# A two-layer hybrid block in fp32: order of the query projection, query transposes, start of the fill, and where the norm's sums of squares are kept

## The chip, the cores and the metric

One core of one Trainium2 chip runs the whole program. The metric is the device time of one execution in microseconds, the median over the runs of the kernel.

## The reference

Two layers run one after the other over 512 latent tokens and 256 context tokens of width 1024. Each layer makes a modulated RMS norm, one input projection whose columns go to three groups of heads, one output projection, and a gated feed-forward network:

```python
hx = ada_modulate(x, norm_mix, sh_m, sc_m)            # rms_norm(x)*gain*(1+scale)+shift
hc = ada_modulate(cx, norm_mix, csh_m, csc_m)
fx, nqx, nkx, nvx, gqx, gkx, gvx, ggx, gax = split_in(hx @ w_in)
y_fn = fourier_mix(fx, fnet_w)                        # Re(2-D DFT) per 64 channels, then @ fnet_w
qxh, kxh, vxh = rms_norm(heads(nqx), na_q_norm), rms_norm(heads(nkx), na_k_norm), heads(nvx)
y_na = na_latent(qxh, kxh, vxh, kch, vch, na_rpb)     # 6 heads x 64, window 8x16 on a 64-wide grid + context keys
y_gla, yc_gla = gla_mix(...)                          # gated linear attention, 4 heads, both directions
y = jnp.concatenate([y_fn, y_na, y_gla], axis=-1) @ w_out
x = x + g_m * y
x = x + g_f * swiglu(ada_modulate(x, norm_ffn, sh_f, sc_f), ffn_w1, ffn_w3, ffn_w2)
```

The context stream goes through the same steps in layer 0 alone (its queries see only context keys); the output is the latent stream after layer 1.

## The kernel before

Everything is fp32. A product of two fp32 operands is three matmuls, since each operand is split into a high and a low part (`mm3`, line 181: high by high, low by high, high by low). Weights come from memory as `raw` and are split into `whl` by ScalarE and VectorE or GpSimd (lines 195 and 189), eight row blocks of 128 for a width of 1024.

A layer goes through these stages, with one order of matmuls for each:

- **Input projections.** `group(...)` runs a token tile of 128 at a time through one group of columns, and hands the PSUM bank to an evacuation function. The last four calls (lines 821 to 824) make the gate g of the linear attention and k, v, q of the neighbourhood attention; `ev_scr` (line 720) evacuates them and stores each tile to a scratch in DRAM by SP (line 732). For g that is a tanh and two products, for v one ScalarE copy, for k and q the head norm of lines 704 to 718: square on ScalarE (`hsq`), sum over a head and a small scaling on VectorE (`hss`), the power of -1/2 on GpSimd (`hrs`), two multiplications on VectorE (`nst`). In layer 0 q has six tiles (latent and context), in layer 1 four. The modulation vectors of what follows (`adac`, line 192) are made on VectorE during the same time. A last projection (lines 827 to 853) makes the input of the Fourier part.
- **Front of the attention.** `load_heads` (line 879) loads k, then q, then v back from the scratch in the order of the window's blocks, as `kn`, `qn`, `vn`. `fourier()` (line 1032) makes the DFT. `stacks_of_heads` (line 908) transposes the first two heads of kn and then of qn on TensorE (line 924) and splits them into the stacks `st` on ScalarE and VectorE. It is called once (line 1119), after six (layer 1: three) steps of `fourier()`; the rest of the Fourier steps come behind it in the program, and the scheduler weaves the two together.
- **Attention.** The loop of lines 1270 to 1298 writes TensorE's order out by hand. A unit is a pair of heads and a block of 128 queries: 15 units in layer 0 (3 pairs, 5 blocks), 12 in layer 1 (3 pairs, 4 blocks). For each, the scores of unit n are issued, then the transposes of unit n-1's probabilities (line 1223), then `fill`, then pieces of the next pair's transposes (line 947), then the values of unit n-1. The softmax in between is VectorE's biased maximum (`mx`, line 1191), ScalarE's exponential, VectorE's reciprocal (`rcl`, line 1201) and scaling.
- **The fill.** `fill(us)` issues pieces of `wo`, the part of the output projection that doesn't depend on the attention: 3 matmuls a piece, one row of 5 row blocks, in layer 1 8 x 5 = 40 pieces of 512 columns. It holds a credit: each call adds 2.4 us in layer 0 or 2.3 in layer 1, and pieces are issued while the credit is positive, each taking off columns x 3 / 2400 us. The credit starts at -2.4, so nothing is issued at the first unit. What is left of `wo` at the end is issued before the rest of the output projection.
- **Output projection of the attention and the norm behind it.** `wb` (line 1265) adds the attention's part of the output projection and the gated residual, a stream and a row block at a time. After each, `norm_add` (line 363) squares the new row block on ScalarE (`nsq`) and adds it to the stream's running sum `nacc` in SBUF: for the first stream (layer 0: the 256 context tokens; layer 1: the first half of 256 latent tokens) on VectorE, for the second (layer 0: the 512 latent tokens; layer 1: the second half) on GpSimd. `norm_sums` makes the column sums by matmuls with ones (`a<-u,nacc`), then `nms`, the power `nrs` on GpSimd, the spread over the partitions (`ndg`), and the modulation (`nt`, `u`) for the feed-forward network, whose first matmuls are `b<-u,whl` and `a<-u,whl`.

TensorE's order is written out by hand in the attention and the output projection; elsewhere a scheduler fixes each engine's order at build time by the order of the program and its own priorities. DMA is issued by SP, one queue in program order.

Of the kernel before, what the change touches and what calls it, by code (L numbers as in the profile page):

```python
# [19 lines left out]
AF = mybir.ActivationFunctionType  # L20
ALU = mybir.AluOpType
# [4 lines left out]
KD = 8  # L26
# [116 lines left out]
def hybrid_kernel(tc, d, out, dbg=None):  # L143
    nc = tc.nc
    ctx = ExitStack()
    V, S, G, T = nc.vector, nc.scalar, nc.gpsimd, nc.tensor
# [41 lines left out]
    def tt(e, o, a, b, op):  # L188
        e.tensor_tensor(out=o, in0=a, in1=b, op=op)  # L189
# [4 lines left out]
    def act(o, i, f=AF.Identity, **kw):  # L194
        S.activation(out=o, in_=i, func=f, **kw)  # L195
# [164 lines left out]

        return products, finish

    def norm_add(acc, x, k, tp, e):

        if k == 0:
            act(acc, x, AF.Square)
            return
        sq = mk(tp, [128, TL], F32, "nsq", 2)[:, :x.shape[-1]]
        act(sq, x, AF.Square)
        tt(e, acc, acc, sq, ALU.add)  # L370

    def norm_acc(xs, n, tp, e):

# [77 lines left out]
    for l in range(DEPTH):  # L451
# [108 lines left out]
        def group(src, cols, specs, evac, together=0, w=None, ps=None, after=None):  # L560

            w = w or wgroup(src, cols)
            ps = ps or {}
            for n, (i, c0) in enumerate(specs):
                if n == len(specs) - together:
                    for m, (j, cj) in enumerate(specs[n:]):
                        ps[j] = dense("mbmbya")[:, :cols - cj]  # L570
                    for k in range(KD):
                        for j, cj in specs[n:]:
                            token_major(ps[j], w, j, cj, k)
                if i not in ps:
                    ps[i] = dense("mb" if l == 0 else "mbmby")[:, :cols - c0]
                    for k in range(KD):
                        token_major(ps[i], w, i, c0, k)
                tick()
                evac(i, ps[i])
                next(steps, None)  # L580
                next(steps, None)
                if after:
                    after()
# [236 lines left out]

        group(d["wg"][l, 1], 384, qonly, ev_scr("g"))
        group(d["wg"][l, 2], 384, both, ev_scr("k"), after=between)
        group(d["wg"][l, 3], 384, both, ev_scr("v"), after=between)
        group(d["wg"][l, 4], 384, qonly, ev_scr("q"), after=between)


        ze = [mk(zp, [128, 2, 258], F32R) for _ in range(2)]
# [80 lines left out]
        def stacks_of_heads(p):  # L908

            for src, gain in ((kn, None), (qn, qg)):  # L910
                n = 768 if ctx_q or gain is None else 512
                kinds = (0, 1) if gain is None else (2,)
                for hh in range(2):
                    for k in kinds:
                        stacks[0, hh, k] = mk(p, [128, n], F32R, f"st{hh}{k}")
                for (j0, nj) in ((0, 4), (4, 2)):
                    if src is qn and j0 and not ctx_q:
                        continue
                    c0 = 128 * j0 if src is qn else (128 * j0 + 256) % 768
                    sl = slice(c0, c0 + 128 * nj)  # L920
                    pss = [ps()[:, :128 * nj] for ps in (PB, PA)]
                    for j in range(nj):
                        for hh, ps in enumerate(pss):
                            T.transpose(ps[:, 128 * j:128 * j + 128], src[j0 + j][:, 128 * hh:128 * hh + 128], ident)
                    for hh, ps in enumerate(pss):
                        u = [stacks[0, hh, k][:, sl] for k in kinds]
                        if gain is None:
                            split(ps, u[0], u[1])
                        else:
                            act(u[0], ps, AF.Copy, scale=gain)  # L930
                            lo = u[0][64:128]
                            stt(lo, ps[64:128], gain[64:128], lo.bitcast(F32), ALU.mult, ALU.subtract)
# [182 lines left out]
        load_heads(nap, "v", vn)  # L1115
        for _ in range(6 if ctx_q else 3):
            next(fn)
        with tc.issue_after(last_mm[0]):
            stacks_of_heads(nap)
        for _ in fn:  # L1120
            pass
        fst.close()
# [11 lines left out]

        load_streams(range(3))

        credit = [-2.4]

        def fill(us):

# [159 lines left out]
        nst_ = ExitStack()  # L1300
        np0 = pool(nst_, f"fn{l}", "left")
        accs = [mk(np0, [128, TL], F32, "nacc", 2)[:, :st_[1](0).shape[-1]] for st_ in streams]
        engines = (V, G) if ctx_q else (V, G)
        with tc.manual_schedule(engines={mybir.EngineType.PE}):
            since = 0
            for mn, _ in wb:
                if mn is None:
                    continue
                m, n = mn
                norm_add(accs[n], streams[n][1](m), m, np0, engines[n])  # L1310
                if mn == (1, 0):
                    early_w = tc.cur_priority
                if since == (1 if ctx_q else 3):
                    sums = norm_sums((accs[0], accs[0].shape[-1]), np0)
                if since == (2 if ctx_q else 7):
                    rb = norm_spread(sums, np0)
                since += bool(since) or mn == (KD - 1, 0)
# [142 lines left out]
```

## Time and profile before

| what | value |
|---|---|
| median of three runs | 1687.62 us (1684.39 to 2008.04) |
| the profiled execution | 1687.75 us |
| its span (first to last instruction) | 1686.0 us |
| granted clock of TensorE, mean | 0.984 of 2.4 GHz |
| busy: PE, VectorE (DVE), ScalarE (ACT), GpSimd (POOL) | 1634.9, 925.9, 581.4, 236.9 us |
| read from and written to memory | 174.84 and 14.29 MB |

The difference between the execution and its span, 1.75 us, lies outside of the profiled instructions. The program is a single run through the two layers: layer 0's attention begins at about 290 us, layer 1's at about 1205 us. How long a matmul takes is seen in the trace at two levels of the granted clock, 1.0 (2.4 GHz) and 0.5 (1.2 GHz); a window's clock is the mean over it. In a timeline, a row's bracket holds the idle time of the engine just ahead of it and what released it. The mark u in names of tiles stands for several unnamed tiles: identity, ones, halves of an operand.

### The profile page before, as it was taken

The page shows a single profiled execution, that of the slowest core. Times are in us where ns is not written, and L with a number is a line of the kernel's source. Part 1 is how long each engine was busy: PE and PEld are TensorE (multiplying, and loading weights), DVE is VectorE, ACT ScalarE, POOL GpSimd, SP SyncE. Part 2 cuts the span into 40 slices and gives each one's busy share as a digit, 9 for nine tenths or more (in the row PEclk, how much of TensorE's full clock was granted, in tenths as well). Part 3 has the DMA queues.
Part 4 walks back from the last instruction along what each step waited for, and adds up shares of the span by engine and source line. Part 5 has one row for each costly group of instructions (what it writes and reads, how often), then busy time and mean ns, then how long its engine had stood idle before and what let it go on. Part 6 is the DMA issues. An engine that isn't in the chain of part 4 may idle for free.

```text
span 1686.0 us, 25086 instructions
## 1 busy us (share of the span) xinstructions
PE 1634.9 (97%) x9938; PEld 1415.1 (84%) x9938; DVE 925.9 (55%) x1680; ACT 581.4 (34%) x1030; POOL 236.9 (14%) x280
## 2 busy tenths in 40 slices
PE   6999999999999999999999999999899999999999
PEld 5888898787888888888888889899777888888887
DVE  6799875677755553454533443453577553344332
ACT  4474224444334311221122324832444432222220
POOL 0243331003212300000000011332102200000000
PEclk9999999999899999999999999999899999999999
DMA  9445535634133352342321311222763143223321
GB/s 339 156 153 166 185 104 170 186 91 133 41 122 124 119 186 96 126 153 85 125 63 55 120 46 40 94 91 73 202 166 111 51 138 100 95 86 107 100 86 52
DMA packets 79906, 199.68 MB, mean 118 GB/s; under 512 B 10344, under 2 KB 21164, under 8 KB 78764
## 3 DMA queue, kind: packets, MB, share of 16 engines
q1 hardware_dynamic: 79788, 198.07, 37.3%
q8 instruction: 78, 1.28, 0.3%
q14 instruction: 40, 0.33, 0.1%
HBM read 174.84 MB, written 14.29 MB: 112 GB/s over the span
## 4 chain that ended last, share of the span: by engine, by line
PE 87%; DMA 5%; DVE 3%; ACT 2%; issue 1%; SPq 1%; POOL 1%; ACTq 0%; DVEq 0%; POOLq 0%
PE a L181 29%; PE m L181 25%; PE b L181 21%; PE y L181 10%; PE b L1223 1%; DMA qn<-scr_q 1%; DVE u L192 1%; DVE whl L189 1%; DMA st<-qt 1%; DMA raw<-in_woa 1%; DMA kn<-scr_k 0%; DMA bias<-in_rpb 0%; DVE nacc L189 0%; DMA raw<-in_wg 0%; ACT ab L195 0%
## 5 line engine op out<-in xcount | busy, mean ns | idle before, releaser
L195 ACT ACTIVATE whl<-raw 128x1024 fp32r<-128x1024 f32 (+7 forms) x222 | 204.8, 928 | 386.3 <-PE a L181 140.0
L181 PE MATMUL m<-u,whl 128*128 128x512 f32 (+1 forms) x1278 | 264.8, 359 | 0.5 <-DVE whl L189 0.5
L189 DVE TENSOR_TENSOR whl<-raw,whl 128x1024 fp32r<-128x1024 f32 (+7 forms) x201 | 223.1, 1112 | 73.7 <-ACT whl L195 73.6
L181 PE MATMUL a<-u,whl 128*128 128x512 f32 (+1 forms) x1299 | 249.0, 348 | 2.9 <-ACT u L195 2.4
L181 PEld LDWEIGHTS m<-u,whl 128*128 128x128 f32 x1278 | 212.7, 192 | 33.8 <-issue 1.2
L181 PEld LDWEIGHTS a<-u,whl 128*128 128x128 f32 x1299 | 210.5, 191 | 34.4 <-ACT u L195 2.8
L181 PE MATMUL b<-u,whl 128*128 128x512 f32 (+1 forms) x915 | 184.9, 352 | 3.1 <-DVE whl L189 1.8
L181 PEld LDWEIGHTS b<-u,whl 128*128 128x128 f32 x915 | 152.2, 193 | 26.7 <-DVE whl L189 2.4
L192 DVE SCALAR_TENSOR_TENSOR adac<-adaw,u,adac 128x512 f32<-128x512 f32 x196 | 154.6, 810 | 35.9 <-DMA adaw<-in_adaw 34.5
L181 PE MATMUL b<-whl,u 128*128 128x384 f32 (+1 forms) x696 | 145.6, 344 | 1.8 <-DVE u L192 1.8
L181 PE MATMUL m<-whl,u 128*128 128x384 f32 (+2 forms) x672 | 139.7, 344 | 1.9 <-ACT u L195 1.9
L181 PEld LDWEIGHTS m<-whl,u 128*128 128x128 f32 x672 | 115.6, 188 | 16.3 <-issue 9.6
L181 PEld LDWEIGHTS b<-whl,u 128*128 128x128 f32 x696 | 121.6, 188 | 8.0 <-issue 3.3
L181 PE MATMUL a<-g,whl 128*128 128x512 f32 (+1 forms) x594 | 126.7, 370 | 0.0
L181 PEld LDWEIGHTS a<-g,whl 128*128 128x128 f32 x594 | 103.9, 189 | 19.4 <-DVE ft L192 0.8
L192 DVE SCALAR_TENSOR_TENSOR ft<-ft,a 128x512 f32<-128x512 f32 (+1 forms) x53 | 30.5, 575 | 99.7 <-ACT ft L195 65.2
L181 PE MATMUL y<-u,whl 128*128 128x512 f32 (+1 forms) x420 | 82.5, 349 | 0.1
L181 PEld LDWEIGHTS y<-u,whl 128*128 128x128 f32 x420 | 68.1, 189 | 12.1 <-issue 1.7
L181 PE MATMUL m<-g,whl 128*128 128x512 f32 (+1 forms) x396 | 77.8, 350 | 0.0
L189 POOL TENSOR_TENSOR nacc<-nacc,nsq 128x256 f32<-128x256 f32 (+1 forms) x21 | 21.0, 1002 | 391.4 <-ACT nsq L195 391.3
L181 PEld LDWEIGHTS m<-g,whl 128*128 128x128 f32 x396 | 64.7, 189 | 9.7
L181 PE MATMUL b<-g,whl 128*128 128x256 f32 (+1 forms) x396 | 72.5, 336 | 0.0
(217 smaller groups left out, 2015.2 us busy)
## 6 DMA issues: line engine op xcount, KB each, us to landing
raw<-in_w SPq DMA_DIRECT2D x104, 512.0 KB
adaw<-in_adaw SPq DMA_DIRECT2D x48, 512.0 KB
adaw<-in_adaw SPq DMA_DIRECT2D x64, 256.0 KB
raw<-in_wg SPq DMA_DIRECT2D x40, 384.0 KB
raw<-in_w SPq DMA_DIRECT2D x32, 448.0 KB
adaw<-in_ada SPq DMA_DIRECT2D x8, 1024.0 KB
st<-kt SPq DMA_DIRECT2D x32, 192.0 KB
raw<-in_woa SPq DMA_DIRECT2D x16, 320.0 KB
```

Source lines behind the costliest of these rows:

```text
L181: last_mm[0] = T.matmul(o, lhsT=l, rhs=r, start=start, stop=stop, skip_group_check=True).ins
L189: e.tensor_tensor(out=o, in0=a, in1=b, op=op)
L192: V.scalar_tensor_tensor(out=o, in0=a, scalar=s, in1=b, op0=op0, op1=op1)
L195: S.activation(out=o, in_=i, func=f, **kw)
L1223: T.transpose(ps[:, 128 * j:128 * j + 128], p[:, 128 * j:128 * j + 128], ident)
```

## The change

Four edits are made.

1. q is projected ahead of v. The call of `after=between`, which advances the linear attention's output by a step, goes along with each tile.
2. `stacks_of_heads` becomes a generator with a stop ahead of k and one ahead of q. The stacks of k are made where both were; two more steps of `fourier()` follow; then the stacks of q; then the rest of `fourier()`.
3. The credit of `fill` starts at 0.
4. The running sum of squares of the first stream (both streams in layer 1) is held in one PSUM bank and added up by VectorE; the last of the eight additions writes the sum to SBUF, where the matmul with ones reads it. In layer 0 the latent stream's sum stays with GpSimd in SBUF.

```diff
--- before.py
+++ after.py
@@ -360,14 +360,15 @@
 
         return products, finish
 
-    def norm_add(acc, x, k, tp, e):
-
+    def norm_add(acc, x, k, tp, e, ps=None):
+
+        part = acc if ps is None else ps
         if k == 0:
-            act(acc, x, AF.Square)
+            act(part, x, AF.Square)
             return
         sq = mk(tp, [128, TL], F32, "nsq", 2)[:, :x.shape[-1]]
         act(sq, x, AF.Square)
-        tt(e, acc, acc, sq, ALU.add)
+        tt(e, acc if k == KD - 1 else part, part, sq, ALU.add)
 
     def norm_acc(xs, n, tp, e):
 
@@ -820,8 +821,8 @@
 
         group(d["wg"][l, 1], 384, qonly, ev_scr("g"))
         group(d["wg"][l, 2], 384, both, ev_scr("k"), after=between)
+        group(d["wg"][l, 4], 384, qonly, ev_scr("q"), after=between)
         group(d["wg"][l, 3], 384, both, ev_scr("v"), after=between)
-        group(d["wg"][l, 4], 384, qonly, ev_scr("q"), after=between)
 
 
         ze = [mk(zp, [128, 2, 258], F32R) for _ in range(2)]
@@ -908,6 +909,7 @@
         def stacks_of_heads(p):
 
             for src, gain in ((kn, None), (qn, qg)):
+                yield
                 n = 768 if ctx_q or gain is None else 512
                 kinds = (0, 1) if gain is None else (2,)
                 for hh in range(2):
@@ -1115,8 +1117,15 @@
         load_heads(nap, "v", vn)
         for _ in range(6 if ctx_q else 3):
             next(fn)
+        first = stacks_of_heads(nap)
+        next(first)
         with tc.issue_after(last_mm[0]):
-            stacks_of_heads(nap)
+            next(first)
+        for _ in range(2):
+            next(fn)
+        with tc.issue_after(last_mm[0]):
+            for _ in first:
+                pass
         for _ in fn:
             pass
         fst.close()
@@ -1134,7 +1143,7 @@
 
         load_streams(range(3))
 
-        credit = [-2.4]
+        credit = [0.0]
 
         def fill(us):
 
@@ -1300,14 +1309,15 @@
         nst_ = ExitStack()
         np0 = pool(nst_, f"fn{l}", "left")
         accs = [mk(np0, [128, TL], F32, "nacc", 2)[:, :st_[1](0).shape[-1]] for st_ in streams]
-        engines = (V, G) if ctx_q else (V, G)
+        bank = PA()
+        sums_ps = (bank[:, 0:256], None) if ctx_q else (bank[:, 0:256], bank[:, 256:512])
         with tc.manual_schedule(engines={mybir.EngineType.PE}):
             since = 0
             for mn, _ in wb:
                 if mn is None:
                     continue
                 m, n = mn
-                norm_add(accs[n], streams[n][1](m), m, np0, engines[n])
+                norm_add(accs[n], streams[n][1](m), m, np0, V if sums_ps[n] is not None else G, sums_ps[n])
                 if mn == (1, 0):
                     early_w = tc.cur_priority
                 if since == (1 if ctx_q else 3):
```

TensorE around the front of layer 0's attention, before; `kn` and `qn` in the input are transposes for the stacks, `m<-whl,ab` and `y<-u,u` matmuls of the Fourier part, `a<-st,st` scores, `b<-u,p` transposes of the probabilities, `m<-u,whl` the fill.

```order
L924 MATMUL a_3327<-u_104,qn_625_3103 128x128
...
L924 MATMUL b_3300<-u_104,kn_619_3091 128x128
...
L181 MATMUL m_3360<-whl_3253,ab_663_3277 128x258
...
L181 MATMUL y_3350<-u_3174,u_2893 1x256 x3
...
L924 MATMUL b_3326<-u_104,qn_625_3103 128x128
...
L181 MATMUL m_3360<-u_3259,ab_681_3357 128x258 x2
...
L181 MATMUL m_3384<-u_3259,ab_681_3357 128x258 x2
...
L181 MATMUL m_3384<-whl_3256,ab_665_3293 128x256 x3
L181 MATMUL a_3441<-st_666_3296,st_674_3324 128x512
...
L181 MATMUL a_3484<-st_666_3296,st_674_3324 128x512
...
L1223 MATMUL b_3512<-u_104,p_3452 128x128 x4
...
L181 MATMUL m_3531<-u_3055,whl_3088 128x256 x9
```

The same place after the change:

```order
L926 MATMUL b_3300<-u_104,kn_622_3097 128x128
...
L926 MATMUL b_3314<-u_104,kn_623_3099 128x128
...
L181 MATMUL m_3384<-u_3259,ab_675_3331 128x258
...
L926 MATMUL b_3360<-u_104,qn_625_3103 128x128
L926 MATMUL a_3361<-u_104,qn_625_3103 128x128
...
L181 MATMUL m_3384<-u_3259,ab_675_3331 128x258 x2
...
L181 MATMUL a_3441<-st_666_3296,st_679_3358 128x512
...
L181 MATMUL m_3480<-u_3055,whl_3088 128x256 x9
...
L181 MATMUL m_3497<-u_3054,whl_3088 128x512 x6
...
L181 MATMUL a_3513<-st_666_3296,st_679_3358 128x512
...
L1232 MATMUL b_3541<-u_104,p_3452 128x128 x4
```

The qn transposes now stand behind the Fourier stage's matmuls into the first of the two banks, eight matmuls ahead of the first scores, and the fill stands between the first scores and the second, where before it followed the first transposes of probabilities.

SP's queue at the end of layer 1's projections, before (`scr_v` and `scr_q` are the scratches in DRAM, `kn` and `qn` the loads from them, `in_dftl` and `in_woa` tables and weights):

```order
L732 DMA scr_v_1539_9368<-nst_11109 128x384
...
L732 DMA scr_q_1540_9369<-nst_11191 128x512
...
L732 DMA scr_q_1540_9369<-nst_11263 128x512
...
L426 DMA raw_11462<-in_dftl 128x514
...
L1073 DMA pe_11526<-in_nyq 1x258
L732 DMA scr_q_1540_9369<-nst_11299 128x512
L888 DMA kn_1929_11441<-scr_k_1538_9367 128x1x512
...
L886 DMA kn_1933_11449<-scr_k_1538_9367 128x512
...
L426 DMA raw_11434<-in_woa 128x640
...
L890 DMA qn_1935_11453<-scr_q_1540_9369 128x1x512
```

The same place after the change:

```order
L733 DMA scr_q_1541_9370<-nst_11026 128x512
...
L733 DMA scr_v_1540_9369<-nst_11116 128x384
...
L733 DMA scr_v_1540_9369<-nst_11280 128x384
L427 DMA raw_11330<-in_wfx 128x512
...
L733 DMA scr_v_1540_9369<-nst_11308 128x384
L427 DMA raw_11463<-in_dftl 128x514
...
L1075 DMA pe_11527<-in_nyq 1x258
L889 DMA kn_1930_11442<-scr_k_1539_9368 128x1x512
...
L887 DMA kn_1934_11450<-scr_k_1539_9368 128x512
...
L427 DMA raw_11435<-in_woa 128x640
...
L891 DMA qn_1936_11454<-scr_q_1541_9370 128x1x512
```

The last store ahead of the loads of kn is now one of v; the stores of q are all further up.

VectorE in layer 1's norm, before (`nacc`: the running sum in SBUF; `nms`, `ndg`, `nt`: the steps behind it):

```order
L189 TENSOR_TENSOR nacc_12648<-nacc_12648,nsq_12668 128x256
...
L189 TENSOR_TENSOR nacc_12648<-nacc_12648,nsq_12675 128x256
...
L192 SCALAR_TENSOR_TENSOR u_11670<-y_12734,u_107,u_11670 128x256
...
L189 TENSOR_TENSOR nacc_12648<-nacc_12648,nsq_12731 128x256
L192 SCALAR_TENSOR_TENSOR u_11671<-a_12746,u_107,u_11671 128x256
...
L391 TENSOR_SCALAR nms_12777<-a_12774 128x2
...
L189 TENSOR_TENSOR whl_13209<-raw_13207,whl_13209 128x1024
...
L403 TENSOR_SCALAR ndg_12838<-u_104,nrs_12779 128x128
```

The same place after the change; `a_12651` is the PSUM bank of the sums:

```order
L189 TENSOR_TENSOR a_12651<-a_12651,nsq_12670 128x256
...
L189 TENSOR_TENSOR a_12651<-a_12651,nsq_12677 128x256
...
L192 SCALAR_TENSOR_TENSOR u_11671<-y_12736,u_107,u_11671 128x256
L189 TENSOR_TENSOR nacc_12649<-a_12651,nsq_12733 128x256
...
L189 TENSOR_TENSOR a_12651<-a_12651,nsq_12759 128x256
...
L189 TENSOR_TENSOR a_12651<-a_12651,nsq_12773 128x256
...
L189 TENSOR_TENSOR a_12651<-a_12651,nsq_12794 128x256
...
L192 SCALAR_TENSOR_TENSOR nt_12905<-u_11671,u_109,a_12839 128x256
...
L189 TENSOR_TENSOR a_12651<-a_12651,nsq_12808 128x256
L192 SCALAR_TENSOR_TENSOR u_12877<-nt_12905,u_107,u_12877 128x256
...
L189 TENSOR_TENSOR nacc_12650<-a_12651,nsq_12857 128x256
```

The first half's additions keep their places; those of the second half, which stood on GpSimd, now stand among the steps of the first half's modulation (`ndg`, `nt`, `u`), three of them ahead of `nt`.

## Rows read from the trace of the kernel before

**Rows 1.** The page: granted clock in 40 slices; shares of the chain that ended last.

```profile
PEclk9999999999899999999999999999899999999999
...
PE 87%; DMA 5%; DVE 3%; ACT 2%; issue 1%; SPq 1%; POOL 1%; ACTq 0%; DVEq 0%; POOLq 0%
```

**Rows 2.** Window by stage: busy us and instructions of each engine, granted clock, DMA share, GB/s.

```profile
185.00:230.00 45.00, 45.00 (x306) 40.17 (x306) 36.03 (x72) 9.64 (x18) 12.41 (x9) 1.00 0.57 178
```

**Rows 3.** Timeline of PE, 289 to 313 us: start, duration, instruction, idle before and releaser.

```profile
289.74 0.33 PE L924 MATMUL a<-u,qn 128*128 128x128 f32 x1 [1.56 <-DMA qn<-scr_q]
...
298.92 0.98 PE L181 MATMUL m<-whl,ab 128*128 128x256 f32 x6
...
305.79 2.16 PE L1223 MATMUL b<-u,p 128*128 128x128 f32 x8 [1.78 <-DVE rcl L1201]
...
307.60 5.40 PE L181 MATMUL m<-u,whl 128*128 128x256 f32 x21
```

**Rows 4.** Window of the attention's front in layer 0.

```profile
288.00:314.00 26.00, 20.08 (x112) 16.34 (x111) 15.04 (x37) 11.02 (x27) 1.76 (x6) 0.80 0.54 167
```

**Rows 5.** Timeline of PE, 1205 to 1229 us, layer 1.

```profile
1205.34 0.30 PE L924 MATMUL a<-u,qn 128*128 128x128 f32 x1 [2.57 <-DMA qn<-scr_q]
...
1217.63 2.08 PE L181 MATMUL a<-st,st 128*128 128x512 f32 x4 [1.57 <-DVE st L192]
...
1223.29 2.15 PE L1223 MATMUL b<-u,p 128*128 128x128 f32 x8 [1.02 <-DVE rcl L1201]
...
1225.09 3.79 PE L181 MATMUL m<-u,whl 128*128 128x512 f32 x12
```

**Rows 6.** Window of the attention's front in layer 1.

```profile
1204.00:1229.00 25.00, 20.16 (x72) 14.89 (x72) 13.63 (x33) 9.09 (x23) 1.20 (x4) 0.59 0.56 168
```

**Rows 7.** Timeline of DVE and SP around the last store of q, layer 1.

```profile
1183.97 0.55 DVE L709 TENSOR_REDUCE hss<-hsq 128x6 f32<-128x384 f32 x1 [0.91 <-ACT hsq L195]
...
1186.46 0.76 DVE L189 TENSOR_TENSOR nst<-y,hrs 128x256 f32<-128x256 f32 x2 [1.50 <-POOL raw L848]
...
1187.24 0.35 SPq L732 DMA_DIRECT2D scr_q<-nst  x1
...
1187.64 2.54 SPq L888 DMA_DIRECT2D kn<-scr_k  x4
```

**Rows 8.** Timelines of DVE, POOL and PE in layer 1's norm, and its window.

```profile
1300.67 4.94 POOL L189 TENSOR_TENSOR whl<-raw,whl 128x1024 fp32r<-128x1024 f32 x2 [0.40 <-ACT whl L195]
...
1303.67 2.22 DVE L189 TENSOR_TENSOR nacc<-nacc,nsq 128x256 f32<-128x256 f32 x1
...
1306.21 0.41 DVE L189 TENSOR_TENSOR nacc<-nacc,nsq 128x256 f32<-128x256 f32 x1
...
1308.65 0.98 PE L181 MATMUL a<-u,nacc 128*128 128x1 f32 x4 [2.33 <-DVE nacc L189]
...
1319.09 0.51 PE L181 MATMUL b<-u,whl 128*128 128x256 f32 x2 [0.87 <-ACT u L195]
...
1308.00:1317.00 9.00, 8.35 (x45) 8.35 (x46) 4.90 (x12) 5.00 (x9) 6.87 (x7) 0.62 0.40 138
```

**Rows 9.** Layer 0's norm: timelines of PE and DVE, one group of lines, one window.

```profile
407.06 1.21 PE L181 MATMUL a<-u,whl 128*128 128x256 f32 x8 [0.22 <-DVE whl L189]
...
421.56 2.08 PE L181 MATMUL b<-u,whl 128*128 128x256 f32 x8 [1.13 <-DVE whl L189]
...
395.49 0.42 DVE L189 TENSOR_TENSOR u<-y,u 128x256 fp32r<-128x256 f32 x1 [2.36 <-ACT u L195]
...
404.90 2.10 DVE L189 TENSOR_TENSOR whl<-raw,whl 128x384 fp32r<-128x384 f32 x1
...
L189 DVE TENSOR_TENSOR nacc<-nacc,nsq 128x256 f32<-128x256 f32 x7 | 7.3, 1043 | 3.5 <-ACT nsq L195 3.5
...
420.00:428.00 8.00, 6.83 (x29) 5.85 (x30) 4.72 (x10) 2.10 (x4) 2.20 (x4) 0.79 0.00 0
```

**Rows 10.** Timeline of PE, last fill of layer 1.

```profile
1287.87 2.99 PE L181 MATMUL m<-u,whl 128*128 128x512 f32 x12
```

## The prediction

> **What bounds the kernel now.** I read the page first. TensorE carries 87% of the chain that ended last [rows 1], so only three things can shorten the program: PE's remaining idle time, the time that it spends at the lower clock, and its work. The change takes no work from PE (same matmuls, other order). The line PEclk of the slices shows where the clock was lowered: slice 11 and slice 29, one place in each layer. Then I read the windows by stage, the way to see which stage has slack: in the queries' and values' projections of layer 0 (185 to 230 us) PE is busy for all of 45.00 us and VectorE for 36.03 [rows 2]; the windows of the two fronts and the two norms are taken up below. Last came the timelines of PE, DVE and SP at the four places that the change touches: the front of the attention in each layer, and the norm behind it in each layer.
>
> **Front of attention, layer 0.** PE stops four times between 288 and 314 us, first 1.56 us for a load of qn, last 1.78 us for the softmax (rcl); the fill of 21 matmuls, which takes 5.40 us there, could have stood in these gaps, but starts only behind the last of them, at 307.60 [rows 3]. The window shows 20.08 us busy of 26.00 at a granted clock of 0.80 [rows 4]: 2.4 GHz for most of it, 1.2 GHz for stretches behind the stops. At the full clock this work is 20.08 x 0.80 = 16.1 us, so the most that can be had is 26.0 - 16.1 = 9.9: 5.9 of idle, 4.0 of clock. On PE the change moves 6 transposes of kn and 28 small matmuls of the Fourier stage ahead of the 12 transposes of qn; six such matmuls take 0.98 us [rows 3], so this is some 4 to 5 us of work, against 1.56 us and a second wait of about 1 for the load, and the start credit of 0 lets 21 fill matmuls run right behind the first scores, which covers the softmax waits. What is late next: the first scores now follow the transposes by only 8 matmuls, some 1.3 us, where 16 stood before, and need the split of the same stacks, which cost a bare wait of 1.57 us in layer 1 [rows 5]. I put about 1 us there. If the loads of qn still land too late, only the softmax waits and their share of the clock go, about half of the 9.9, or 5. Ends 5 and 9.9; value 8, near the row's own total less the new wait.
>
> **Front of attention, layer 1.** The same, deeper: stops of 2.57 (qn), 1.57 (st), 1.02 (rcl) and two small ones, then the fill's 12 matmuls take 3.79 us, where 12 of the same form take 2.99 at full clock later on [rows 5, 10]. The window 1204 to 1229 has 20.16 us busy of 25.00 at a clock of 0.59 [rows 6], so 11.9 us of work and at most 13.1 us to gain. Here the loads decide. The stores of q close the projections: behind the last product stand square, sum (hss 0.55), POOL's power and two multiplications (0.76 us) before the store of q at 1187.24, and SP issues the first load of kn only behind it, at 1187.64 [rows 7]. With v last, one ScalarE copy stands there, so kn, and qn behind it, can start about 3 us sooner, and q was stored long before. On PE the qn transposes also move back, by some 2.6 us of work. The waits of 2.57 and two small ones for qn ended with the last load near 1210 us, so 3 + 2.6 us covers most of it and not surely all. The wait of 1.57 for the split stays, since the scores still stand right behind the transposes. So at best 13.1 - 1.6 - 0.5 = 11. If the kn loads are held by something else than the store (they reuse memory of the stage before), the wait is only renamed, the clock falls again, and about 5.1 is left. Ends 5.1 and 11; value 8.5, between.
>
> **Norm behind the attention, layer 1.** VectorE's adds of squares run at 2.22 us while GpSimd runs weight splits of 2.5 us each (4.94 for two), and at 0.41 when it doesn't; PE waits 2.33 us for the last of them, and the window 1308 to 1317 then has a clock of 0.62 [rows 8]. That is 2.33 + 8.35 x 0.38 = 5.5 us. With the sum in PSUM the add should cost what a VectorE operation with one PSUM operand of the same size costs, 0.42 [rows 9], also beside GpSimd. Against that, the seven adds of the second half move from GpSimd to VectorE (7 x 0.42 = 2.9), and by the order three of them now stand ahead of the first modulated tile, on which the feed-forward's first matmul waits already for 0.87 us [rows 8]: 1.3 us later. Lower end 0 (the adds wait for ScalarE's square anyway, or PSUM adds are no faster), upper 5.5; value 4.0.
>
> **Norm behind the attention, layer 0.** Only the context's sum moves (7 adds of 128x256). Before, they take 7.3 us, the group's sum, where 7 x 0.42 = 2.9 would do, and five PE waits of 0.22 to 1.13 us, 2.9 together, all behind VectorE's or ScalarE's weight splits, follow; the window 420 to 428 has 6.83 busy at 0.79, another 1.4 [rows 9]. Ends 0 and 4.3; value 2.3, since part of the delay is the weight splits' own: one of 128x384 took 2.10 us [rows 9], while GpSimd was busy, and the latent stream's sum stays on GpSimd in SBUF. The Trainium skill's page "SBUF — State Buffer", section "Who interferes with whom", says that a VectorE operation with two SBUF inputs and a GpSimd operation that reads SBUF block each other for a whole instruction, and one with a single SBUF input does not. The trace agrees for the adds (2.22 against 0.41). The rule speaks against the full gain here: the splits have two SBUF inputs and keep their GpSimd neighbour. By it the term would be about 1.2, and the sum 1.1 less.
>
> **What the change costs.** (1) The fill has 0 for its start, so it is used up sooner. Layer 1 has 40 pieces of 0.64 us by the kernel's own count, 25.6 in all, and 12 blocks that ask for 2.3 each from the first on, 27.6; so they are gone one block early, and the 12 matmuls (2.99 us) that stand between the last scores and the last values [rows 10] are missing there: PE waits for the last softmax, about 2 us, with a drop of the clock possible. Ends 1 and 5; value 2. Layer 0 loses its last 9 matmuls ahead of the output projection, and waits for the split that ends with the 0.42 us operation at 395.49 [rows 9]: 0.5, ends 0 and 1. (2) In layer 0 six head norms of q (hss and two multiplications, 0.55 + 0.76, with the small scaling about 1.45 us on VectorE each) come into 185 to 230 us: 36.0 + 8.7 = 44.7 of 45.0 us [rows 2, 7]. That nothing waits rests on this being just enough. Ends 0 and 3; value 0.8. (3) SP: the last store moves by three places and four loads of qn start sooner: nothing.
>
> **Sum.** 8 + 8.5 + 4.0 + 2.3 - 2 - 0.5 - 0.8 = 19.5 us. The profiled execution took 1687.75 (span 1686.0 and 1.75 around it), 0.13 over the median of 1687.62. 1687.6 - 19.5 = 1668.1.
>
> **Rivals.**
> A, the waits are renamed. The loads of qn and kn end as late as now, PE stands at the moved transposes, and the clock falls there. For it: both fronts show DMA as releaser of the first stop; the landings in layer 1 go on to about 1210. Against it: in layer 0 the transposes move further than the stop was long. Both fronts at their lower ends: 5 + 5.1 + 6.3 - 3.3 = 13.1, so 1674.5.
> B, the norms give nothing. Each add waits for ScalarE's square, and in layer 1 the seven extra adds keep VectorE as late as it was. For it: VectorE stood idle for 3.5 us ahead of layer 0's seven adds, all of it behind a square [rows 9]. Against it: the 2.22 us adds of layer 1 had their squares long before. 8 + 8.5 - 3.3 = 13.2, less 1 for the late modulation: 1675.4.
> C, slower than before. VectorE in 185 to 230 us has 0.3 us of slack left and is fed by loads and by ScalarE, so it cannot fill every gap: the modulation of the next stage and the head norms fall behind, PE's banks are not emptied, and PE, which now never stops there, stands for the whole 8.7 us, then runs at 1.2 GHz for some 20 us (10 us lost), and the late q pushes back the front of the attention, whose 8 us then don't come. 19.5 - 8 - 8.7 - 10 + 0.8 = -6.4: 1694. It decides once VectorE's lag costs PE over 5 us, because then the clock goes too. For it: 44.7 of 45. Against it: from 230 us on VectorE is lightly used, and the next stage's modulation can slip there.
>
> **How the numbers follow.** Forecast 0.58, A 0.24, B 0.12, C 0.06. The forecast's own range is 1668 with about 8 to each side from the ends of the two fronts. Range for all: 1654 (both fronts and the norms near their upper ends, 9.9 + 11 + 9.8 - 1 = 29.7, which would be 1658, and some more for clock that I counted in no term) to 1684 (A and B together give 6.8, less a clock drop at the end of layer 1, 3). 2% of the time, about what a measurement of this kernel can tell from no change, is 33.8 us, which is more than all upper ends together: faster 0.05, within 0.92, slower 0.03 (C with more than one stretch at the lower clock).
>
> **What would show it.** Right: PEclk near 9 in slices 11 and 29; no wait for qn and rcl on PE at either front; fill matmuls straight behind the first scores; layer 1's adds at about 0.42 beside GpSimd's splits and no stop of 2.33 us ahead of the sums' matmuls; a wait of 1 to 3 us for p or rcl in layer 1's last block. Wrong: PE idle in layer 0 between 185 and 230 us (C); a stop at the moved transposes with DMA as releaser (A); adds still at 1 us or more, or a longer stop at the first feed-forward matmul (B).

## Result, and the profile after

The kernel after the change takes 1667.43 us (median of four runs, 1664.77 to 1668.75), 0.9888 of the kernel before, with a 95% interval of 0.9868 to 0.9909; the ratio leaves out the one slow run of the kernel before, at 2008.04 us. By that ratio it is 18.9 us faster, 15.3 to 22.3; run once more as a control beside the experiments it came to 0.9898 [0.9878, 0.9919]. The profiled execution took 1666.35 us, its span is 1664.3. The forecast was 1668.1.

The page after, against [rows 1]: no slice of PEclk is below 9 any more. (The chain of the page is not compared: it breaks off early in this trace and covers some 30% of the span.)

```profile
PE   6999999999999999999999999999999999999999
...
PEclk9999999999999999999999999999999999999999
```

The windows after, moved to where the same work now stands: the projections of q and v in layer 0, the front in each layer, then the norm in layer 1 and in layer 0, against [rows 2, 4, 6, 8, 9].

```profile
185.00:230.00 45.00, 45.00 (x305) 39.92 (x305) 42.05 (x95) 10.08 (x19) 19.47 (x15) 1.00 0.59 190
286.00:312.00 26.00, 22.03 (x141) 18.46 (x140) 16.48 (x41) 12.09 (x30) 1.76 (x6) 0.93 0.65 198
1191.00:1216.00 25.00, 21.11 (x125) 17.20 (x126) 18.10 (x39) 13.51 (x31) 0.86 (x4) 0.93 0.67 195
1289.00:1298.00 9.00, 7.47 (x61) 7.06 (x60) 8.01 (x20) 5.27 (x11) 2.24 (x2) 1.00 0.70 227
414.00:422.00 8.00, 7.33 (x44) 6.29 (x43) 5.75 (x13) 3.19 (x7) 3.56 (x3) 1.00 0.09 32
```

Most of what the fronts gained is clock: 0.80 to 0.93 and 0.59 to 0.93. Idle time fell less, from 5.9 to 4.0 us in layer 0 and from 4.8 to 3.9 in layer 1. The timelines say where it stands. Layer 0's front, PE and then DVE; the first row lies ahead of the window:

```profile
283.95 0.33 PE L926 MATMUL a<-u,kn 128*128 128x128 f32 x1 [0.96 <-DMA kn<-scr_k]
...
297.62 1.25 PE L181 MATMUL a<-st,st 128*128 128x512 f32 x4
298.70 3.42 PE L181 MATMUL m<-u,whl 128*128 128x256 f32 x21
...
302.32 1.17 PE L181 MATMUL a<-st,st 128*128 128x512 f32 x4
307.16 1.00 PE L1232 MATMUL b<-u,p 128*128 128x128 f32 x4 [3.67 <-DVE p L1211]
```

```profile
303.24 0.69 DVE L189 TENSOR_TENSOR kt<-b,kt 128x512 fp32r<-128x512 f32 x1 [0.20 <-ACT kt L195]
305.56 0.48 DVE L192 SCALAR_TENSOR_TENSOR u<-m,u,u 128x256 f32<-128x256 f32 x1 [1.63 <-DMA u<-in_cxt]
305.96 0.15 DVE L1210 RECIPROCAL rcl<-sml 128x1 f32<-128x1 f32 x1
```

The two stops for qn are gone, and the fill of 21 matmuls stands right behind the first scores as written, in 3.42 us where it took 5.40 [rows 3]. But a new stop of 3.67 us follows, and a transpose of kn now waits 0.96 us for its load, which none did before. Read the DVE rows: the residual addition of the fill's own first product (`u<-m,u,u`) waits 1.63 us for a load of the context stream, and the reciprocal of the softmax, which PE waits for, stands behind it in VectorE's queue.

Layer 1's front, PE, then DVE and SP:

```profile
1171.90 3.39 PE L181 MATMUL y<-whl,u 128*128 128x384 f32 x18
...
1198.86 0.90 PE L926 MATMUL a<-u,qn 128*128 128x128 f32 x4
...
1204.38 1.55 PE L181 MATMUL a<-st,st 128*128 128x512 f32 x4 [2.83 <-DVE st L192]
```

```profile
1176.89 0.33 SPq L733 DMA_DIRECT2D scr_v<-nst  x1
1177.61 0.81 SPq L427 DMA_DIRECT2D raw<-in_dftl  x2
...
1178.84 1.30 SPq L889 DMA_DIRECT2D kn<-scr_k  x2
...
1202.79 0.75 DVE L189 TENSOR_TENSOR raw<-pe,m 128x255 f32<-128x255 f32 x2
1203.57 0.76 DVE L192 SCALAR_TENSOR_TENSOR st<-b,qg,st 64x512 fp32r<-64x512 f32 x1
```

No transpose of qn waits any more. The split ahead of the first scores, 1.57 us in [rows 5], costs 2.83 now: VectorE still does two operations of the Fourier stage (`raw<-pe,m`) ahead of it, and PE has no work in its order in between. The first row is the last product of the projections; in the kernel before it is this one, and the first load of kn stands at 1187.64 [rows 7]:

```profile
1179.38 3.39 PE L181 MATMUL y<-whl,u 128*128 128x384 f32 x18
```

The norms: the adds in layer 1 as a group of lines, then PE in layer 1 and layer 0 with what it waits for.

```profile
L189 DVE TENSOR_TENSOR a<-a,nsq 128x256 f32<-128x256 f32 x12 | 5.1, 427 | 0.2
```

```profile
400.56 7.74 POOL L189 TENSOR_TENSOR whl<-raw,whl 128x1024 fp32r<-128x1024 f32 x3 [2.56 <-ACT whl L195]
400.93 2.42 DVE L189 TENSOR_TENSOR whl<-raw,whl 128x384 fp32r<-128x384 f32 x1 [0.86 <-ACT whl L195]
403.40 1.21 PE L181 MATMUL m<-u,whl 128*128 128x256 f32 x8 [1.67 <-DVE whl L189]
...
1289.30 0.50 PE L181 MATMUL a<-u,nacc 128*128 128x1 f32 x4
...
1297.15 0.50 PE L181 MATMUL b<-u,whl 128*128 128x256 f32 x2 [1.41 <-ACT u L195]
```

Twelve adds at 0.427 us on the mean, none at 2.2 [rows 8]; the stop of 2.33 us is gone, the one at the first feed-forward matmul grew from 0.87 to 1.41. In layer 0 a weight split under GpSimd's splits takes 2.42 us (0.55 where GpSimd stands idle) and still stops PE for 1.67, as the 2.10 us split of [rows 9] let one expect.

The two ends of the fill, first layer 0's, where the output projection begins, then the values of the last block but one in layer 1:

```profile
395.07 1.33 PE L181 MATMUL y<-u,whl 128*128 128x256 f32 x9 [0.95 <-DVE u L189]
...
1272.99 1.56 PE L181 MATMUL y<-pT,vn 128*64 128x128 f32 x16 [0.31 <-ACT pT L195]
```

### The profile page after: what moved, and what is told of

It is laid out like the page before. It is cut to its first block, busy times and chain, and to the rows that moved or that the text cites. A ratio compares the mean times of both kernels' runs of the same rounds, so it can differ in the third digit from the quotient of the medians.

```text
span 1664.3 us, 25086 instructions
## 1 busy us (share of the span) xinstructions
PE 1620.0 (97%) x9938; PEld 1403.3 (84%) x9938; DVE 920.3 (55%) x1687; ACT 581.1 (35%) x1030; POOL 230.5 (14%) x273
## 5 line engine op out<-in xcount | busy, mean ns | idle before, releaser
L181 PEld LDWEIGHTS b<-g,whl 128*128 128x128 f32 x396 | 61.5, 190 | 8.6 <-issue 0.8
```

The costliest lines, as they stand in the source:

```text
L181: last_mm[0] = T.matmul(o, lhsT=l, rhs=r, start=start, stop=stop, skip_group_check=True).ins
```

## Experiments

All ratios are to the kernel before. Since several theories are about one stage, the profiled executions were also cut at the same places: from layer 0's first Fourier transposes (`b<-u,gv`) over the first scores to the first matmul of the attention's output projection (F0); from there to the first matmul of the norm's second spread over the partitions (N0); the same two in layer 1 (F1, N1). The table gives how many us shorter each stretch is than in the profiled execution of the kernel before (123.1, 42.4, 99.1 and 38.7 us there).

| kernel | edits | ratio and 95% interval | F0 | N0 | F1 | N1 |
|---|---|---|---|---|---|---|
| after | 1 2 3 4 | 0.9888 [0.9868, 0.9909] | 3.2 | 3.3 | 9.6 | 4.6 |
| control | 1 2 3 4 | 0.9898 [0.9878, 0.9919] | 2.6 | 3.3 | 11.4 | 4.4 |
| e1_norm | 4 | 0.9974 [0.9964, 0.9985] | 1.9 | 2.6 | 2.2 | 4.4 |
| e2_credit | 3 | 0.9970 [0.9953, 0.9987] | 1.4 | -0.5 | 5.5 | 1.0 |
| e3_qfirst | 1 | 0.9954 [0.9937, 0.9970] | 0.2 | 0.9 | 1.7 | 0.6 |
| e4_order | 1 2 | 0.9940 [0.9916, 0.9963] | 3.5 | 2.2 | 6.8 | 0.0 |
| e8_no_late | 1 3 4 | 0.9925 [0.9900, 0.9950] | 1.4 | 2.1 | 7.5 | 4.6 |
| e7_credit_l1 | 1 2 4, 3 in layer 1 | 0.9914 [0.9899, 0.9930] | 4.0 | 2.6 | 9.1 | 3.0 |
| e6_sbuf | 1 2 3 | 0.9945 [0.9929, 0.9962] | 2.7 | -0.9 | 11.4 | 0.8 |
| e5_v_behind_x | all, and vn behind x | 0.9884 [0.9870, 0.9899] | 5.6 | 3.1 | 8.0 | 4.5 |
| e9_fill_ahead | e5, and a fill ahead | 0.9895 [0.9868, 0.9921] | 5.2 | 3.1 | 8.5 | 4.8 |

A stretch whose code is the same differs between executions. F0 and F1 of e1_norm, whose fronts are those of before, read 1.9 and 2.2; F1 of the five kernels with one and the same attention in layer 1 (after, control, e5, e6, e7) lies between 8.0 and 11.4; N0 of the five without edit 4 between -0.9 and 2.2, and N1 of the seven with it between 3.0 and 4.8. So a difference of 2 us, in F1 and N0 of 3, in a single trace shows nothing.

**e1_norm: edit 4 alone.** The kernel before with the parts of the diff in `norm_add` and behind `bank = PA()`.

> Kernel before with edit 4 alone (sums of squares in PSUM). Theory (the sum is worth what the prediction gave it and a little more): in layer 1 the stop of 2.33 us ahead of the sums' matmuls goes and the clock behind it stays at 1.0, the first half's adds take about 0.42 us beside GpSimd's splits; in layer 0 the adds take 0.42 us each, but a stop behind a weight split stays. The time falls by 6 to 8 us. Rival (the adds wait for ScalarE's squares anyway): under 2 us.

4.4 us faster, 2.5 to 6.1 by the interval. In the trace the stop ahead of the sums is gone and no add in layer 1 takes over 0.43 us; N1 gained 4.4 and N0 2.6. The time came to less than the 6 to 8 expected, and less than the two stretches together; the rival, under 2, falls.

**e2_credit: edit 3 alone.**

```diff
-        credit = [-2.4]
+        credit = [0.0]
```

> Kernel before with edit 3 alone (the fill's credit starts at 0). Theory (VectorE is blocked in program order: the residual add of the first fill product waits for the load of x and stands ahead of the softmax's reciprocal): in layer 0 a stop of 2 us or more remains ahead of the first transposes of probabilities, so the early fill gives under 2 us there; in layer 1, where qn stops PE before, the clock stays low; the time changes by -2 to +2 us. Rival (the fill covers the softmax waits, as the prediction has it): 3.3 us of waits and some 2 us of clock less in layer 0, 1 us in layer 1, less 2.5 at the ends: 3 to 4 us faster.

5.1 us faster, 2.2 to 7.9: more than the theory's 2 at most. The rival's 3 to 4 lie inside the interval, but by the stretches the gain is in the other layer than the rival has it. In layer 0 the fill covers the softmax in part (stops of 0.72 and 1.16 us in place of 1.54 and 1.78), but the first add doesn't wait for the load, because the scores start some 4 us later (301.79 in place of 297.62), behind the stops for qn:

```profile
292.00 0.33 PE L924 MATMUL a<-u,qn 128*128 128x128 f32 x1 [1.88 <-DMA qn<-scr_q]
...
308.16 0.66 PE L1223 MATMUL b<-u,p 128*128 128x128 f32 x4 [0.72 <-DVE p L1202]
```

F0 gained no more than e1_norm's unchanged front did; F1 gained 5.5, where e1_norm's read 2.2. So VectorE's block is no property of the early fill alone: it needs the early scores too.

**e3_qfirst: edit 1 alone.** The two `group` calls exchanged.

> Kernel before with edit 1 alone (q projected ahead of v). Theory: in layer 1 the first load of kn follows the last projection by about 3.6 us in place of 4.9, so 1.3 us sooner, and the stops for qn, 3.5 us together, shrink but don't go: 1 to 4 us faster; in layer 0 the stops for qn stay as they are, and PE is busy throughout 185 to 230 us. Rival 1 (the loads are held by memory that they reuse and not by the store): no change. Rival 2 (VectorE falls behind with the head norms in 185 to 230 us): PE idle there, 5 us slower or more.

5 to 11 us faster by the interval, 7.8 by the ratio; but its profiled execution was the slowest of its four (1682.38 us, where the other three took 1676.2 to 1676.7), and its stretches show 1.7 us in F1 at most. In it the loads of kn start 3.02 us behind the last product, in place of 4.87, and yet the stops for qn in layer 1 are still there, 1.9 us together:

```profile
1201.87 0.33 PE L924 MATMUL a<-u,qn 128*128 128x128 f32 x1 [0.61 <-DMA qn<-scr_q]
```

That is less than the 3.5 us in the trace of before, but it lies between the 2.3 of e1_norm and the 1.7 of e2_credit, which lack edit 1. So it is not shown that edit 1 shrinks them.

Layer 0's stops for qn stayed (1.41 and 0.91 us). PE is busy for 45.00 of 45.00 us from 185 to 230, with VectorE at 40.13: rival 2 falls, and with the sooner loads and the shorter time rival 1 too. Where the rest of the 7.8 us is, this trace can't show.

**e8_no_late: the kernel after, with both stacks made together again.**

```diff
-        first = stacks_of_heads(nap)
-        next(first)
-        with tc.issue_after(last_mm[0]):
-            next(first)
-        for _ in range(2):
-            next(fn)
         with tc.issue_after(last_mm[0]):
-            for _ in first:
+            for _ in stacks_of_heads(nap):
                 pass
```

> Kernel after with edit 2 undone (both stacks made together again, edits 1, 3 and 4 kept). Theory (the transposes of qn have to move back as well as the loads forward): stops for qn with DMA as releaser come back, some 2.5 us in layer 0 and 1 to 3 us in layer 1, and the clock falls in both fronts: 4 to 9 us slower than the kernel after, so 12 to 16 us faster than before. Rival (the place of the transposes matters little, the loads' earlier start is enough): within 2 us of the kernel after.

0.9925, so some 12.6 us faster than before and 4.5 to 6 slower than the control and the kernel after, with intervals that overlap theirs. The stops for qn are back in both layers, 1.32 and 0.99 us in layer 0 and three of 0.42 to 0.62 in layer 1, and the clock is lower: the window of the front in layer 1, 1190 to 1230 us, has 0.87, against 0.96 in the kernel after. The first of the stops:

```profile
291.99 0.33 PE L926 MATMUL a<-u,qn 128*128 128x128 f32 x1 [1.32 <-DMA qn<-scr_q]
```

As to the stops the theory holds: the loads' earlier start alone doesn't take them away. Its price in time is not clear of the noise.

**e4_order: edits 1 and 2.** The kernel before with the `group` calls exchanged and the generator.

> Kernel before with edits 1 and 2 (q ahead of v, qn's transposes later); fill and norms as before. Theory (the loads' start and the transposes' place together remove the stops for qn, the other two edits are separate): no stop for qn in either front; the softmax stops of 1 to 2 us stay in layer 0, and a stop of 2.8 us for the split ahead of the first scores stands in layer 1; 8 to 12 us faster than before. Rival (without the early fill the clock stays down in the fronts): under 5 us.

10.1 us faster (6.2 to 14.2). No transpose of qn waits in either front. The split's stop ahead of layer 1's first scores is there, to the digit:

```profile
301.43 1.20 PE L181 MATMUL a<-st,st 128*128 128x512 f32 x2 [2.72 <-DVE mx L1199]
303.85 2.25 PE L1231 MATMUL b<-u,p 128*128 128x128 f32 x8 [1.22 <-DVE p L1210]
...
1204.61 1.19 PE L181 MATMUL a<-st,st 128*128 128x512 f32 x4 [2.83 <-DVE st L192]
```

That is the largest single part of the change, and it stands without the other two edits. How the 10.1 us divide between edits 1 and 2 the times don't show, since the intervals of e3_qfirst and e4_order overlap; the stops for qn are gone only where edit 2 is in. No run has edit 2 without edit 1, so whether it needs edit 1 stays open. One more window of this run, over the part of layer 0's norm that ran at 0.79 before [rows 9]; edit 4 is not in it:

```profile
414.00:422.00 8.00, 6.72 (x38) 5.34 (x37) 5.96 (x11) 3.03 (x6) 3.36 (x3) 1.00 0.12 38
```

**e7_credit_l1: the kernel after, with the fill's old start in layer 0.**

```diff
-        credit = [0.0]
+        credit = [-2.4 if ctx_q else 0.0]
```

> Kernel after with the old start of the credit, -2.4, in layer 0 only. Theory (the early fill gives almost nothing in layer 0, since its first residual add blocks VectorE): the stop of 3.67 us is replaced by two softmax stops of 1 to 2 us, 3 us together; within 1.5 us of the kernel after. Rival (the early fill is worth in layer 0 what the prediction gave it): 4 to 6 us slower than the kernel after.

0.9914, 2.7 us slower than the control by the ratios, with intervals that overlap. F0 is no longer than in the kernel after (4.0 against 3.2 and 2.6): the stop of 3.67 us has become two,

```profile
302.02 0.73 PE L181 MATMUL a<-st,st 128*128 128x512 f32 x2 [2.72 <-DVE mx L1200]
304.44 2.25 PE L1232 MATMUL b<-u,p 128*128 128x128 f32 x8 [1.68 <-DVE p L1211]
```

4.4 us together. So by F0 the early fill is worth nothing in layer 0 as it stands, as the theory has it. The time alone doesn't decide: 2.7 us lie between the theory's 1.5 and the rival's 4 to 6.

**e5_v_behind_x: the block taken away.** In layer 0 the loads of vn are issued behind those of x.

```diff
-        load_heads(nap, "v", vn)
+        if not ctx_q:
+            load_heads(nap, "v", vn)
...
         load_streams(range(3))
+        if ctx_q:
+            with tc.issue_after(last_x[0]):
+                load_heads(nap, "v", vn)
```

(`last_x[0]` is the last load that `load_streams` issued.)

> Kernel after; in layer 0 the loads of vn are issued behind the first loads of x and of the context stream instead of ahead of them. Theory (the stop of 3.67 us is VectorE blocked by a residual add that waits for the load of the context stream): the add starts without waiting, the stop shrinks to 1.5 us or less, and the drop of the clock behind it goes: 2 to 4 us faster than the kernel after. Rival (the stop is the softmax's own length): the stop stays at 3 us or more, or the values' matmuls wait for vn as long.

```profile
302.56 0.47 DVE L192 SCALAR_TENSOR_TENSOR u<-m,u,u 128x256 f32<-128x256 f32 x1
302.95 0.15 DVE L1216 RECIPROCAL rcl<-sml 128x1 f32<-128x1 f32 x1
...
304.16 0.66 PE L1238 MATMUL b<-u,p 128*128 128x128 f32 x4 [1.94 <-DVE p L1217]
305.31 1.09 PE L1238 MATMUL b<-u,p 128*128 128x128 f32 x4 [0.50 <-DVE rcl L1216]
```

The addition has no wait in its row and the stop of 3.67 us (3.45 in the control) is 1.94 and 0.50; F0 gains 2.4 to 3.0 us over the kernel after and the control. So the wait for the load was the cause of a part of the stop, 1.2 us of 3.67. What remains is the softmax itself, so half of the rival was right as well. The time, 1665.28 us and 0.9884, is 1.3 us under the control's 1666.57, too little to tell apart with these runs.

**e6_sbuf: the sums in SBUF, GpSimd without additions in layer 1.**

```diff
-        sums_ps = (bank[:, 0:256], None) if ctx_q else (bank[:, 0:256], bank[:, 256:512])
+        sums_ps = (None, None)
...
-                norm_add(..., V if sums_ps[n] is not None else G, sums_ps[n])
+                norm_add(..., (V, G if ctx_q else V)[n], None)
```

> Kernel after with the sums of squares in SBUF again (layer 0 as before: VectorE and GpSimd; layer 1: both on VectorE, so GpSimd adds nothing). Theory (two SBUF inputs: VectorE's add and GpSimd's weight split hold each other up): the first half's adds in layer 1 take about 2 us beside a split and PE stops 2 us ahead of the sums, with the clock down behind it; 5 to 8 us slower than the kernel after. Rival (the gain in layer 1 came from taking the adds off GpSimd): layer 1 as in the kernel after, 2 to 3 us slower from layer 0 alone.

```profile
1286.51 4.95 POOL L189 TENSOR_TENSOR whl<-raw,whl 128x1024 fp32r<-128x1024 f32 x2 [0.45 <-ACT whl L195]
...
1289.51 2.23 DVE L189 TENSOR_TENSOR nacc<-nacc,nsq 128x256 f32<-128x256 f32 x1
...
1294.50 0.60 PE L181 MATMUL a<-u,nacc 128*128 128x1 f32 x4 [2.39 <-DVE nacc L189]
```

7.9 us slower than the control by the ratios. With the additions off GpSimd but in SBUF, the 2.23 us add, the split beside it and PE's stop of 2.39 us stand as before the change: in layer 1 it is the place of the sum, not the engine that adds the second half. N1 falls from 4.4 to 0.8, N0 from 3.3 to -0.9.

**e9_fill_ahead: work for the gap of 2.83 us.** e5_v_behind_x, and

```diff
+                    if n == 0 and not ctx_q:
+                        fill(2.3)
                     pairs[pr].scores(b)
...
-                fill(2.4 if ctx_q else 2.3)
+                fill(2.4 if ctx_q else 2.1)
```

> The variant with vn behind x in layer 0, and in layer 1 one more fill of 2.3 us ahead of the first scores, with 2.1 in place of 2.3 for each block after. Theory (the stop of 2.83 us is the split's way through ScalarE's and VectorE's queues behind the Fourier stage's last operations, during which PE has nothing in its order): the 12 fill matmuls stand in that gap, the stop shrinks to under 0.5 us, and the fill ends one block early as in the kernel after: 2 to 3 us faster than the kernel after with its variant, 21 us or more faster than before. Rival (the stop comes back elsewhere, at the softmax behind or in the last blocks that lose their fill): within 1 us of the variant without it.

The rival. The stop ahead of the scores is gone, and one as long stands at the softmax behind them:

```profile
1208.70 0.75 DVE L192 SCALAR_TENSOR_TENSOR u<-m,u,u 128x512 f32<-128x512 f32 x1 [0.91 <-DMA u<-xs]
1211.52 0.83 DVE L189 TENSOR_TENSOR whl<-raw,whl 128x640 fp32r<-128x640 f32 x1 [2.07 <-ACT whl L195]
1212.27 0.16 DVE L1216 RECIPROCAL rcl<-sml 128x1 f32<-128x1 f32 x1
...
1213.09 0.63 PE L1238 MATMUL b<-u,p 128*128 128x128 f32 x4 [2.75 <-DVE rcl L1216]
```

It is layer 0's pattern again: the fill's residual addition, waiting 0.91 us for x, and the split of the fill's next weights, waiting 2.07, both stand ahead of the reciprocal. 0.9895: no gain over the variant without it. No version tried is clearly faster than the kernel after.

## Why the prediction came true, point by point

The time was forecast to within a microsecond. (The prediction took 2% for about what a measurement of this kernel can tell from no change; the interval is 0.2% to either side.) The terms were not all as good; what each measured is taken from the stretches, as the mean of the kernels that have the edits less the mean of those that have none of them there.

- **The norm in layer 1: as forecast.** N1 is 4.3 us on the mean of the seven kernels with edit 4 and 0.5 on that of before and the four others, so 3.9 us, where the prediction took 4.0. The adds take 0.42 to 0.43 us as forecast. The price was seen right and set too high: the first feed-forward matmul waits 1.41 us in place of 0.87, 0.5 more and not 1.3.
- **The norm in layer 0: the size as forecast, the cause not shown.** N0 is 2.9 with edit 4 and 0.3 without, 2.5 us against 2.3; but the single values overlap (2.1 to 3.3 and -0.9 to 2.2). PE's stops fell little, from five with 2.9 us together to 1.67 and 0.67. What went is the low clock, 0.79 became 1.00, and that came back without edit 4 too: in e4_order the same work runs at 1.00. So luck may have a part in this term. The Trainium skill says in "SBUF — State Buffer", section "Who interferes with whom", that a VectorE operation with two SBUF inputs contends with a GpSimd operation that reads SBUF; the trace agrees for the weight splits, which kept their neighbour (2.42 us and the stop of 1.67). Between the 1.2 us that the prediction worked out by it and its own 2.3 these runs can't decide.
- **The front in layer 0: mis-sized.** "Value 8", with 0.5 off for the end. F0 is 2.8 on the mean of the kernel after, the control and e6, and 0.7 on that of the three with the transposes and the fill's start of before (before, e1, e3), so some 2.1 us, below the lower end of 5. Over the whole of F0 PE stood idle for 5.9 us, against 6.0 before; only the granted clock rose, from 0.96 to 0.99. The step that failed is "the start credit of 0 lets 21 fill matmuls run right behind the first scores, which covers the softmax waits". They run there, with the softmax stop of 3.67 us behind them, and bring a residual addition with them, which sits in VectorE's queue ahead of the reciprocal and waits for a load that nobody had needed so early. The prediction counted the moved matmuls and not the instruction that follows a product on another engine. With that load in front (e5 and e9, 5.4 on the mean) the term is 4.7; a softmax stop of 1.94 us is left even then. That the stops for qn would go with the moved transposes held (e4 and e7, which lack the early fill here, read 3.5 and 4.0). The end cost a stop of 0.95 us, not 0.5, in all seven kernels with the early fill in layer 0 and in no other.
- **The front in layer 1: better than forecast.** 8.5 less 2 for the last block. F1 is 9.9 on the mean of the five kernels whose attention in layer 1 is that of the kernel after (after, control, e5, e6, e7), and 1.1 on that of before and e1: 8.8 us. Two sizes were wrong. The loads of kn come 1.3 us sooner, not 3: 3.55 us behind the end of the last product of 128x384 in place of 4.87. The last store itself does come 2.9 us sooner (1.60 in place of 4.47), but the tables' loads now stand in SP's queue between it and the first load. The stops for qn went even so, with the transposes' move (e4; undone in e8, they are back). The early fill seems to have some 3 us of the 8.8: F1 is 9.9 with it and 6.8 in e4 without it, and e2 has 5.5 by it alone; as F1 differs by as much between like executions, that is not shown. And the missing fill of the last block costs one stop of 0.31 us and slower matmuls behind it (16 in 1.56 us, 1.09 in full clock), about 1 us, not 2.
- **The split ahead of the scores.** Forecast as 1.57 us in layer 1 and about 1 in layer 0, it is 2.83 and 0. In layer 0 the fill stands over what is left of it: in e4 and e7, which have no fill there, the next stop, for the maximum, is 2.72 us in place of 1.54. The order of TensorE showed the place, not what VectorE has ahead of the split.
- **VectorE in 185 to 230 us.** Forecast busy for 44.7 of 45 us, it is for 42.05, and PE for 45.00: the price of 0.8 was 0, and rival C has nothing in its favour.
- **Rivals A and B.** No transpose of qn waits in the kernel after, and the adds are at 0.43 us beside GpSimd: both fall. A little of A is there: the stop of 0.96 us for kn in layer 0 (0.90 in the control, 0.86 in e8, none in the other kernels).

The sum by these sizes is 2.1 + 8.8 + 2.5 + 3.9 = 17.3 us, the ratios give 17.2 and 18.9, the prediction 19.5. The edits taken alone add up to much the same, 10.1 (e4), 5.1 (e2) and 4.4 (e1), 19.6 us. So the total was right in part by luck, because a term too large and a term too small stood side by side. Besides, the sum was made against one execution, whose front in layer 1 stopped 3.5 us for qn, where e1_norm and e2_credit, with the same code up to there, stopped for 2.3 and 1.7.

## What to carry to other kernels

Whoever moves matmuls into a gap must list what follows each product on the other engines and which load that needs: an addition that waits in an in-order queue holds back everything behind it, and the gap comes back one step later (layer 0's 3.67 us, e9's 2.75). A running sum that VectorE adds to beside GpSimd's work is worth trying in PSUM; here an add took 2.2 us from SBUF beside a split and 0.43 from PSUM. And the stops for loads differ by a microsecond or two between executions of the same code (3.5, 2.3 and 1.7 us), so a term read from one profile carries that much doubt.

## What was not expected of the hardware

The same stop doesn't always cost the clock. In the kernel after and in its control PE stops for 2.83 us at the same place, ahead of layer 1's first scores; the windows from 1204 to 1210 us, first the kernel after, then the control:

```profile
1204.00:1210.00 6.00, 5.62 (x19) 4.45 (x20) 3.72 (x10) 1.89 (x5) 0.44 (x2) 0.72 0.88 265
```

```profile
1204.00:1210.00 6.00, 5.25 (x26) 4.33 (x27) 4.39 (x11) 2.75 (x6) 0.44 (x2) 1.00 0.92 261
```

The granted clock fell to a mean of 0.72 in the one and stayed at 1.00 in the other, and the 12 fill matmuls behind the stop take 4.18 us and 2.90. So the price of a stop is its length and, in some executions only, a stretch at 1.2 GHz behind it; what decides between the two these runs don't show.
